# Weight-stationary projections of an encoder layer: of each half weight load, first all products of 512 columns, then all of 256

## The chip, the cores and the metric

One Trainium2 chip, one of its cores. The metric is the device time of one execution of the whole program, in microseconds, as the median of several runs; lower is better. The engines of the core are named as the profile names them: PE (TensorE, matrix products), PEld (the loading of PE's stationary operand), DVE (VectorE), ACT (ScalarE), POOL (GpSimd) and SP (SyncE, which issues most DMAs).

## The reference, cut to what matters

One layer of an encoder over 256 positions of width 2048, all in float32: a mixer of two parallel branches (retention and a gated delta rule) behind one wide input projection, a cross-attention into 256 memory tokens, a squared-ReLU feed-forward of width 8192, and a final norm.

```
h = rms_norm(x, norm_mix_g);  x = x + hybrid_mixer(h, ...)        # w_in: 2048 x 18464, w_out: 2048 x 2048
h = rms_norm(x, norm_x_g);    mem_n = rms_norm(mem, norm_mem_g)
x = x + cross_attention(h, mem_n, w_xq, w_xkv, w_xo)
h = rms_norm(x, norm_ffn_g);  x = x + square(relu(h @ w_ff1)) @ w_ff2
return rms_norm(x, norm_final_g)
```

Nearly all of the work is the matrix products `h @ w`.

## The kernel before

**Products in three parts.** Each float32 operand is split into a rounded part (hi) and the rest (lo), and a product is hi·hi + hi·lo + lo·hi. A weight arrives by DMA in a `raw` tile of 1 MB; `fetch` (L104 on) rounds each half of it on ACT into a tile `whi` (L125) and subtracts on DVE into a tile `wlo` (L126). A half is 128 x 1024 numbers. There are three `raw`, three `whi` and three `wlo` buffers, and later in the program one more pair, `whx` and `wlx`, for every fourth half. The activations lie in "quads", tiles `q` of four feature blocks, each with the 256 hi columns and behind them the 256 lo columns (`both`, 512 columns).

**Two ways to multiply.** `chunk` (L153 on) keeps the activations stationary in PE and streams 512 weight columns, three products of 512 columns for each pair (L166 to L168). `with_seven` (its products at L1185) does the same for the second feed-forward matrix. `values_both` (L401 to L403) does it for the first values of the memory. `blocks_in_steps` (L192 on) is the other way: it keeps a 128 x 128 block of weights stationary and streams activations. For each of the 16 feature blocks `kk` and each of its two output blocks `b`, the hi weights meet all 512 columns of `both` (L210: hi·hi and hi·lo side by side, in the two halves of one PSUM bank), and the lo weights meet the 256 hi columns (L211: lo·hi, added to the first half). When all `kk` are done, L220 and L221 add the two halves of the bank. A pair in this document is one product of L210 and the product of L211 that belongs to it: 2 output blocks x 16 `kk` = 32 pairs in a call, 8 pairs in a half load, and 96 calls, so 384 halves and 3072 pairs in the program. The calls compute the keys of the memory (8 calls, over the quads of the memory, about 97 to 191 us), 8192 columns of the input projection (32 calls), the mixer's output projection (8), the queries and the output projection of the cross-attention (8 each), and the first feed-forward matrix (32).

**Order of the work.** The instructions are put in order at build time by a scheduler with a model of time, within priorities: fetches come first, evacuations next, and small work of the mixer is fitted between the projections' products on PE. `step` and `yield` after each half load let other streams put work in. PE, DVE and ACT each run their own instructions in that order.

**Where the operands lie.** `AT_BLOCKS = (56, 0)` shifts the hi half by 56 numbers (224 bytes) inside its tile in `blocks_in_steps` alone; the other callers of `fetch` use (0, 0). In the built program this gives the following starts, as remainders by 256 bytes within a partition: the blocks of `whi` and `whx` that L210 loads lie at 192, those of `wlo` and `wlx` that L211 loads at 224, and the columns of `q` at 224, except for the four quads of the memory (the keys and the values of the memory), whose columns lie at 0. In L1185 and in L137 to L139 of the cross-attention, both operands lie at 224. In L401 to L403 the loaded operand is a quad of the memory, at 0, and the streamed one a weight at 224.

Of the kernel before, what the change touches and what calls it, by code (L numbers as in the profile page):

```python
# [17 lines left out]
P = 128  # L18
D = 2048
S = 256  # L20
NT = S // P
KT = D // P
# [30 lines left out]
def trunk(ctx: ExitStack, tc: tile.TileContext, x_f, mem_f, positions, lead_f, small_f, w_in, ret_gn_g, w_out, w_xq,  # L53
# [3 lines left out]
    act, vec, pool, pe = nc.scalar, nc.vector, nc.gpsimd, nc.tensor  # L57
# [9 lines left out]
    def stream_ps():  # L67
        s0 = psp.tile([P, 512], F32, name="s0", tag="s0", bufs=2)
        s1 = psp.tile([P, 512], F32, name="s1", tag="s1", bufs=2)
        return s0, s1  # L70
# [24 lines left out]
    def step():  # L95
        if steps and next(steps[0], steps) is steps:
            steps.pop(0)
# [6 lines left out]
    def fetch(pieces, k, n, cuts=1, hold=None, at=(0, 0)):  # L104

        raw = wp.tile([P, k * n], F32, name="raw", tag="raw", bufs=3)
        rv = raw.rearrange("p (k n) -> p k n", k=k)
        with tc.high_priority(offset=100000):
            for off, ap in pieces:
                src = ap.rearrange("(k p) n -> p k n", p=P)  # L110
                for c in range(cuts):
                    ks = slice(c * k // cuts, (c + 1) * k // cuts)
                    fetched.append(nc.sync.dma_start(rv[:, ks, off:off + ap.shape[1]], src[:, ks, :]).ins)
            got = []
            for i in range(2):
                if hold:
                    both = hold().both
                    hi, lo = (both[:, a:a + 2, :].rearrange("p a s -> p (a s)") for a in (0, 2))
                else:
                    hi, lo = (h[:, a:a + k * n // 2] for h, a in zip(half_tiles(), at))  # L120
                src = raw[:, i * k * n // 2:(i + 1) * k * n // 2]
                part = k * n // max(cuts, 2)
                for c in range(0, k * n // 2, part):
                    cs = slice(c, c + part)
                    latest["hi"] = act.activation(hi[:, cs], src[:, cs], AF.Copy).ins  # L125
                    latest["lo"] = vec.tensor_sub(lo[:, cs], src[:, cs], hi[:, cs].bitcast(F32)).ins  # L126
                got.append((hi.rearrange("p (k n) -> p k n", n=n), lo.rearrange("p (k n) -> p k n", n=n)))
            latest["raw"] = fetched[-1]
        return got
# [62 lines left out]
    def blocks_in_steps(quads, w, c0, nb, evac, ends=None):  # L192

        k = 16 // nb
        ps = stream_ps()
        n = nb * P
        for g in range(KT // k):  # L200
            halves = fetch([(0, w[g * k * P:(g + 1) * k * P, c0:c0 + n])], k, n, at=AT_BLOCKS)
            for i in range(k):
                kk = g * k + i
                xh, xhl = quads[kk // 4][0][:, kk % 4, :], quads[kk // 4].both[:, kk % 4, :]
                wh, wl = halves[i // (k // 2)]
                for b in range(nb):
                    bs = slice(b * P, (b + 1) * P)
                    lh, ll = wh[:, i % (k // 2), bs], wl[:, i % (k // 2), bs]
                    with tc.issue_after(ends[-1]) if ends else ExitStack():
                        pe.matmul(ps[b], lh, xhl, start=kk == 0, stop=False)  # L210
                        ins = pe.matmul(ps[b][:, :S], ll, xh, start=False, stop=kk == KT - 1).ins  # L211
                if i % (k // 2) == k // 2 - 1:
                    if ends is not None:
                        ends.append(ins)
                    step()
                    yield
        for b in range(nb):
            with tc.high_priority(offset=50000):
                o = sm.tile([P, S], F32, name="bo", tag="bo", bufs=2)
                act.activation(o, ps[b][:, S:], AF.Copy)  # L220
                vec.tensor_add(o, o, ps[b][:, :S])  # L221
                evac(b, o)

    def blocks(*args):
        for _ in blocks_in_steps(*args):
            pass
# [783 lines left out]
    def residual_pass(quads, w, gain, name, loader=None, between=None):  # L1010
# [4 lines left out]
        for b2 in range(8):  # L1015
            xc = loader(b2) if loader else None
            if b2 % 2 == 0:
                nxt.append(quad_b())

            def evac(b, ps, b2=b2, xc=xc):  # L1020
                k = 2 * b2 + b
                vec.tensor_add(rt[:, k, :], ps, xc[:, b, :] if loader else rt[:, k, :])
                g = gains[:, gain + k:gain + k + 1]
                qh, ql = (a[:, k % 4, :] for a in nxt[-1])
                act.activation(qh, rt[:, k, :], AF.Copy, scale=g)
                vec.scalar_tensor_tensor(ql, rt[:, k, :], g, qh.bitcast(F32), op0=ALU.mult, op1=ALU.subtract)
                sq = xa.tile([P, S], F32, name="sq2", tag="sq2", bufs=2)
                act.activation(sq, rt[:, k, :], AF.Square)
                vec.tensor_add(acc, acc, sq)

            if not between or b2 > 1:
                blocks(quads, w, b2 * 256, 2, evac)
                continue
            first_two.append(blocks_in_steps(quads, w, b2 * 256, 2, evac))
            if b2:
                for which in (0, 0, 0, None, 1, 0, 0, 1, 1, 1, 1):
                    if which is None:
                        between()
                    else:
                        next(first_two[which], None)  # L1040
# [20 lines left out]
    for h in range(XH):  # L1061
# [17 lines left out]
        nb = xa.tile([P, NT], F32, name="nb", tag="nb", bufs=2)  # L1079
# [244 lines left out]
    ends = []  # L1324
# [120 lines left out]
```

## Time and profile before

| What | Value |
|---|---|
| median of 3 runs | 2051.8 us (2050.77 to 2052.64) |
| the profiled execution's own time | 2050.97 us |
| its span, first to last instruction | 2049.2 us |
| PE busy | 2038.1 us, 99% of the span |
| DVE, ACT busy | 1542.9 us, 1153.2 us |
| granted PE clock, mean | 0.999 |
| read from HBM | 389.74 MB, 196 GB/s over the span |

Busy times of PE include products that overlap: the record of a product ends after the next has started, since its columns leave the array while the next ones enter. The time that a product takes up on PE is therefore the distance from its start to the next start. The chain of waits lists instructions that set the end, in order of time, with their share of it (start, duration, engine, output tile, line, count), merged where they follow each other; the timeline lists all instructions by start and duration.

### The profile page before, as it was taken

The page shows a single profiled execution, that of the slowest core. Times are in us where ns is not written, and L with a number is a line of the kernel's source. Part 1 is how long each engine was busy: PE and PEld are TensorE (multiplying, and loading weights), DVE is VectorE, ACT ScalarE, POOL GpSimd, SP SyncE. Part 2 cuts the span into 40 slices and gives each one's busy share as a digit, 9 for nine tenths or more (in the row PEclk, how much of TensorE's full clock was granted, in tenths as well). Part 3 has the DMA queues.
Part 4 walks back from the last instruction along what each step waited for, and adds up shares of the span by engine and source line. Part 5 has one row for each costly group of instructions (what it writes and reads, how often), then busy time and mean ns, then how long its engine had stood idle before and what let it go on. Part 6 is the DMA issues. An engine that isn't in the chain of part 4 may idle for free.

```text
span 2049.2 us, 28493 instructions
## 1 busy us (share of the span) xinstructions
PE 2038.1 (99%) x10850; PEld 1756.6 (86%) x10850; DVE 1542.9 (75%) x2433; ACT 1153.2 (56%) x1871; POOL 36.3 (2%) x50
## 2 busy tenths in 40 slices
PE   9999999999999999999999999999999999999998
PEld 8888888988888888888888899888888888888887
DVE  5887788779667875888557666777868887888785
ACT  6655764575457555755446555555545655655554
POOL 0000000000000000000000000000000000000000
PEclk9999999999999999999999999999999999999999
DMA  9679556555555555555467655569657647555662
GB/s 327 204 253 301 185 183 196 164 185 195 187 168 181 194 196 165 184 182 189 156 206 248 191 180 163 173 180 257 219 169 234 219 159 218 200 199 159 220 217 103
DMA packets 329225, 405.24 MB, mean 198 GB/s; under 512 B 34928, under 2 KB 239360, under 8 KB 328960
## 3 DMA queue, kind: packets, MB, share of 16 engines
q1 hardware_dynamic: 328656, 402.74, 61.1%
q8 instruction: 85, 1.39, 0.3%
q10 hardware_dynamic: 432, 0.69, 0.1%
q14 instruction: 52, 0.43, 0.1%
HBM read 389.74 MB, written 11.55 MB: 196 GB/s over the span
## 4 chain that ended last, share of the span: by engine, by line
PE 96%; DMA 1%; DVE 1%; issue 1%; ACT 1%; SPq 0%; POOLq 0%; POOL 0%; DVEq 0%; ACTq 0%
PE s L210 33%; PE s L211 17%; PE s L167 8%; PE s L168 8%; PE s L166 8%; PE b L1185 7%; PE s L1185 6%; PE s L401 1%; PE s L403 1%; PE s L402 1%; PE b L796 1%; PE b L829 1%; PE b L138 0%; DMA raw<-w_ff 0%; PE b L137 0%
## 5 line engine op out<-in xcount | busy, mean ns | idle before, releaser
L210 PE MATMUL s<-q,whi 128*128 128x512 f32 x2816 | 972.6, 391 | 0.8 <-DVE bo L221 0.6
L126 DVE TENSOR_TENSOR wlo<-raw,whi 128x1024 fp32r<-128x1024 f32 x592 | 722.6, 1222 | 294.9 <-ACT whi L125 288.5
L125 ACT ACTIVATE whi<-raw 128x1024 fp32r<-128x1024 f32 x592 | 627.4, 1060 | 518.9 <-PE s L210 189.2
L211 PE MATMUL s<-q,wlo 128*128 128x256 f32 x2816 | 769.3, 280 | 0.7 <-DVE wlo L126 0.6
L210 PEld LDWEIGHTS s<-q,whi 128*128 128x128 f32 x2816 | 520.8, 188 | 102.9 <-DVE bo L221 0.9
L211 PEld LDWEIGHTS s<-q,wlo 128*128 128x128 f32 x2816 | 528.6, 188 | 13.1 <-DVE wlo L126 1.6
L167 PE MATMUL s<-wlo,q 128*128 128x512 f32 x716 | 281.6, 393 | 0.0
L168 PE MATMUL s<-whi,q 128*128 128x512 f32 x716 | 279.3, 390 | 0.0
L166 PE MATMUL s<-whi,q 128*128 128x512 f32 x716 | 258.9, 390 | 0.0
L166 PEld LDWEIGHTS s<-whi,q 128*128 128x128 f32 x716 | 134.3, 188 | 27.9
L168 PEld LDWEIGHTS s<-whi,q 128*128 128x128 f32 x716 | 134.6, 188 | 26.9
L167 PEld LDWEIGHTS s<-wlo,q 128*128 128x128 f32 x716 | 134.6, 188 | 26.7
L220 ACT ACTIVATE bo<-s 128x256 f32<-128x256 f32 x192 | 72.8, 379 | 107.2 <-PE s L211 107.1
L221 DVE TENSOR_TENSOR bo<-bo,s 128x256 f32<-128x256 f32 x192 | 79.9, 416 | 48.6 <-ACT bo L220 48.3
L125 ACT ACTIVATE whx<-raw 128x1024 fp32r<-128x1024 f32 x56 | 59.3, 1059 | 53.7 <-PE s L210 21.9
L210 PE MATMUL s<-q,whx 128*128 128x512 f32 x256 | 89.2, 389 | 0.0
L126 DVE TENSOR_TENSOR wlx<-raw,whx 128x1024 fp32r<-128x1024 f32 x56 | 68.4, 1221 | 24.6 <-ACT whx L125 24.1
L1185 PE MATMUL s<-whi,q 128*128 128x512 f32 x264 | 85.2, 389 | 0.0
L1185 PE MATMUL b<-whi,q 128*128 128x512 f32 x244 | 78.8, 389 | 0.0
L1206 DVE TENSOR_TENSOR wlo<-rt,whi 128x1024 fp32r<-128x1024 f32 x46 | 56.1, 1223 | 23.3 <-ACT whi L1205 22.5
L211 PE MATMUL s<-q,wlx 128*128 128x256 f32 x256 | 70.5, 280 | 0.0
L1205 ACT ACTIVATE whi<-rt 128x1024 fp32r<-128x1024 f32 x46 | 48.8, 1060 | 33.4 <-PE s L1185 15.3
(385 smaller groups left out, 2344.7 us busy)
## 6 DMA issues: line engine op xcount, KB each, us to landing
raw<-w_in SPq DMA_DIRECT2D x143, 1024.0 KB
raw<-w_ff SPq DMA_DIRECT2D x104, 1024.0 KB
raw<-w_xkv SPq DMA_DIRECT2D x29, 1024.0 KB
raw<-w_out SPq DMA_DIRECT2D x16, 1024.0 KB
raw<-w_xq SPq DMA_DIRECT2D x16, 1024.0 KB
raw<-w_xo SPq DMA_DIRECT2D x16, 1024.0 KB
rt<-w_ff SPq DMA_DIRECT2D x12, 1024.0 KB
tr<-w_ff SPq DMA_DIRECT2D x12, 1024.0 KB
```

The lines of the kernel that those rows point to most:

```text
L125: latest["hi"] = act.activation(hi[:, cs], src[:, cs], AF.Copy).ins
L126: latest["lo"] = vec.tensor_sub(lo[:, cs], src[:, cs], hi[:, cs].bitcast(F32)).ins
L166: pe.matmul(o, xh, wh, start=first, stop=False)
L167: pe.matmul(o, xh, wl, start=False, stop=False)
L168: pe.matmul(o, xl, wh, start=False, stop=last)
L210: pe.matmul(ps[b], lh, xhl, start=kk == 0, stop=False)
L211: ins = pe.matmul(ps[b][:, :S], ll, xh, start=False, stop=kk == KT - 1).ins
L220: act.activation(o, ps[b][:, S:], AF.Copy)
L221: vec.tensor_add(o, o, ps[b][:, :S])
L1185: ins = pe.matmul(o, lhs[l], rhs[r], start=key not in opened, stop=last and j == 2, skip_group_check=True).ins
L1205: latest["hi"] = act.activation(hi, raw[:, c:c + 1024], AF.Copy).ins
L1206: latest["lo"] = vec.tensor_sub(lo, raw[:, c:c + 1024], hi.bitcast(F32)).ins
```

## The change

In each half load, the products of L210 for all four `kk` and both `b` now come first (8 products of 512 columns), and then the 8 products of 256 columns with the lo weights. Before, the two alternated. The products are the same and as many, with the same operands in the same tiles at the same places; only their order differs, and the point in the half at which the lo tile is first read and the hi tile last read. The file is one line shorter, so lines behind it are numbered one lower, and both kinds of product now stand in one line, L210.

```diff
-            for i in range(k):
-                kk = g * k + i
-                xh, xhl = quads[kk // 4][0][:, kk % 4, :], quads[kk // 4].both[:, kk % 4, :]
-                wh, wl = halves[i // (k // 2)]
-                for b in range(nb):
-                    bs = slice(b * P, (b + 1) * P)
-                    lh, ll = wh[:, i % (k // 2), bs], wl[:, i % (k // 2), bs]
-                    with tc.issue_after(ends[-1]) if ends else ExitStack():
-                        pe.matmul(ps[b], lh, xhl, start=kk == 0, stop=False)
-                        ins = pe.matmul(ps[b][:, :S], ll, xh, start=False, stop=kk == KT - 1).ins
-                if i % (k // 2) == k // 2 - 1:
-                    if ends is not None:
-                        ends.append(ins)
-                    step()
-                    yield
+            for h in range(2):
+                for part in range(2):
+                    for i in range(k // 2):
+                        kk = (2 * g + h) * k // 2 + i
+                        x = quads[kk // 4][0] if part else quads[kk // 4].both
+                        for b in range(nb):
+                            o = ps[b][:, :S] if part else ps[b]
+                            with tc.issue_after(ends[-1]) if ends else ExitStack():
+                                ins = pe.matmul(o, halves[h][part][:, i, b * P:(b + 1) * P], x[:, kk % 4, :],
+                                                start=kk == 0 and not part, stop=kk == KT - 1 and part == 1).ins
+                if ends is not None:
+                    ends.append(ins)
+                step()
+                yield
```

The order on PE in the last block of the first feed-forward matrix, before (`s0` and `s1` are the banks of its two output blocks):

```order
L210 MATMUL s0_18055<-q_12127,whi_18059 128x512
L211 MATMUL s0_18055<-q_12127,wlo_18060 128x256
L210 MATMUL s1_18056<-q_12127,whi_18059 128x512
L211 MATMUL s1_18056<-q_12127,wlo_18060 128x256
L210 MATMUL s0_18055<-q_12127,whi_18059 128x512
L211 MATMUL s0_18055<-q_12127,wlo_18060 128x256
```

The same place in the changed program, from the fifth product of the half:

```order
L210 MATMUL s0_18055<-q_12127,whi_18059 128x512
L210 MATMUL s1_18056<-q_12127,whi_18059 128x512
L210 MATMUL s0_18055<-q_12127,whi_18059 128x512
L210 MATMUL s1_18056<-q_12127,whi_18059 128x512
L210 MATMUL s0_18055<-q_12127,wlo_18060 128x256
L210 MATMUL s1_18056<-q_12127,wlo_18060 128x256
L210 MATMUL s0_18055<-q_12127,wlo_18060 128x256
L210 MATMUL s1_18056<-q_12127,wlo_18060 128x256
```

A product of 512 columns was followed by one of 256 and the other way round; now seven of eight are followed by one of their own length.

In the mixer, small products stand between those of the projections. Here are, on PE, the Gram products of the first pair of heads (`kh` and `kl` are the hi and lo parts of a head's keys and queries, made by ACT and DVE), before:

```order
L211 MATMUL s1_2076<-q_110,wlo_2126 128x256
L699 MATMUL b_2189<-kh_2185 128x512
L701 MATMUL b_2190<-kh_2185 128x256
L210 MATMUL s0_2276<-q_107,whi_2280 128x512
L211 MATMUL s0_2276<-q_107,wlo_2281 128x256
L210 MATMUL s1_2277<-q_107,whi_2280 128x512
L211 MATMUL s1_2277<-q_107,wlo_2281 128x256
L210 MATMUL s0_2276<-q_107,whi_2280 128x512
L699 MATMUL b_2189<-kl_2186,kh_2185 128x512
```

And in the changed program:

```order
L210 MATMUL s1_2076<-q_110,wlo_2126 128x256
L698 MATMUL b_2189<-kh_2185 128x512
L700 MATMUL b_2190<-kh_2185 128x256
L210 MATMUL s0_2276<-q_107,whi_2280 128x512
L210 MATMUL s1_2277<-q_107,whi_2280 128x512
L210 MATMUL s0_2276<-q_107,whi_2280 128x512
L698 MATMUL b_2189<-kl_2186,kh_2185 128x512
```

The first product that needs `kl` stood behind five products of the projection, and now stands behind three.

## Prediction

> **What bounds the kernel now.** I read the page's first part, then what PE waited for, then the chain of waits for the pace of PE, then the timeline for single products.
>
> ```profile
> PE 2038.1 (99%) x10850; PEld 1756.6 (86%) x10850; DVE 1542.9 (75%) x2433; ACT 1153.2 (56%) x1871; POOL 36.3 (2%) x50
> PEclk9999999999999999999999999999999999999999
> GB/s 327 204 253 301 185 183 196 164 185 195 187 168 181 194 196 165 184 182 189 156 206 248 191 180 163 173 180 257 219 169 234 219 159 218 200 199 159 220 217 103
> L210 PE MATMUL s<-q,whi 128*128 128x512 f32 x2816 | 972.6, 391 | 0.8 <-DVE bo L221 0.6
> L126 DVE TENSOR_TENSOR wlo<-raw,whi 128x1024 fp32r<-128x1024 f32 x592 | 722.6, 1222 | 294.9 <-ACT whi L125 288.5
> L211 PE MATMUL s<-q,wlo 128*128 128x256 f32 x2816 | 769.3, 280 | 0.7 <-DVE wlo L126 0.6
> L210 PE MATMUL s<-q,whx 128*128 128x512 f32 x256 | 89.2, 389 | 0.0
> L211 PE MATMUL s<-q,wlx 128*128 128x256 f32 x256 | 70.5, 280 | 0.0
> ```
>
> PE is busy for 2038.1 of 2049.2 us, and the clock is full in every slice. The 2816 + 256 = 3072 pairs that the change reorders stood idle for 0.8 + 0.7 us together. So nothing that arrives earlier can win more than 1.5 us in these loops, and the question is only whether PE takes the same products at another pace in another order. The mean durations (391 and 280 ns) are no pace, since products overlap. Pace is the distance from start to start.
>
> ```profile
> 1442.61 21.79 PE b L1185 x96
> 1752.21 2.75 PE b L1185 x12
> 1766.02 2.75 PE b L1185 x12
> 22.71 0.47 PE s L401 x2
> 47.91 0.47 PE s L401 x2
> 123.70 0.47 PE s L210 x2
> 129.28 0.47 PE s L210 x2
> ```
>
> These rows of the chain of waits give four paces.
>
> - An unbroken row of 96 products of 512 columns (L1185) takes 21.79 us: 227.0 ns each.
> - From 1752.21 to 1766.02 us lie 12 products of L1185 (2.75 us) and one block of 32 pairs: 13.81 - 2.75 = 11.06 us, or 345.6 ns a pair. Less 227.0 this leaves 118.6 ns for the product of 256. So today an alternating 512 costs what a 512 costs in an unbroken row.
> - From 22.71 to 47.91 us, in the first values of the memory, lie 9 steps of 12 products of 512 columns (two weight pieces, two token halves, three products): 25.20 us / 108 = 233.3 ns each, 6.3 ns more than in L1185, at the same clock and without idle time.
> - From 123.70 to 129.28 us lies half a block of memory keys, 16 pairs in 5.58 us: 348.8 ns, 3.2 ns more than the later pairs.
>
> What differs in the last two is where the operands lie. PE loads the weights of the next product while the current one streams:
>
> ```profile
> 401.30 0.19 PEld L210 LDWEIGHTS s<-q,whi 128*128 128x128 f32 x1
> 401.30 0.28 PE L211 MATMUL s<-q,wlo 128*128 128x256 f32 x1
> 401.42 0.39 PE L210 MATMUL s<-q,whi 128*128 128x512 f32 x1
> ```
>
> The load for the L210 that starts at 401.42 begins at 401.30, with the L211 before it. So each load runs beside a stream of other data. In L1185 the load and the stream beside it start at the same remainder by 256 bytes (224 and 224): 227.0 ns. In L401 they do not (0 and 224): 233.3 ns. In the later pairs, the load beside the 512 is that of `wlo` (224, stream 224: equal); in the memory keys it is 224 against 0: unequal, and slower. My reading is that a load at another remainder slows the 512 beside it by some 6 ns. The tile that does not fit is `whi` at 192, and today it is always loaded beside the short product.
>
> **The change, step by step.** It adds and removes no product, load, rounding or DMA, and moves no tile. What it swaps is which load runs beside which stream. Take a half of 8 pairs in the later calls.
>
> Today, 8 loads of `wlo` (equal) run beside a 512, and 8 loads of `whi` (unequal) beside a 256: 8 x 345.6 = 2764.8 ns.
>
> After, 7 loads of `whi` (unequal) run beside a 512, one of `wlo` (equal) beside the last 512, 7 of `wlo` (equal) beside a 256, and one of `whi` beside the last 256. For a row of 256 with equal remainders there is this stretch of the cross-attention (timeline):
>
> ```profile
> 1172.82 0.28 PE L137 MATMUL b<-kth,qth 128*128 128x256 f32 x1
> 1172.94 0.28 PE L138 MATMUL b<-ktl,qth 128*128 128x256 f32 x1
> 1173.42 0.28 PE L139 MATMUL b<-kth,qtl 128*128 128x256 f32 x1
> 1173.54 0.39 PE L210 MATMUL s<-q,whi 128*128 128x512 f32 x1
> ```
>
> Six products from 1172.82 to 1173.54 us: 120 ns each, 1.4 above the 118.6 of today. The half becomes 7 x 233.3 + 227.0 + 7 x 120 + 118.6 = 2818.7 ns, 53.9 ns more: 44.1 from the 512s and 9.8 from the 256s.
>
> Of the 384 halves, 32 are those of the memory keys, where the streams start at 0: there `wlo` (224) and `whi` (192) are both unequal, so every load is unequal in either order, and I cost these at nothing. Bound: with the full 53.9 ns it would be 1.7 us.
>
> The sum: 352 x 53.9 ns = 19.0 us. The profiled execution took 2050.97 us (span 2049.2), so 2070.0 us; the median of the runs shown lies 0.8 above it, so **2071 us**.
>
> Prices and their bounds. For a 512 with an unequal load the trace has no long row inside these calls. Upper end, the start of a block, where the scheduler already put two 512s, then two 256s:
>
> ```profile
> 1754.57 0.40 PE L1185 MATMUL b<-whx,q 128*128 128x512 f32 x1
> 1754.81 0.63 PE L210 MATMUL s<-q,whi 128*128 128x512 f32 x2
> 1755.27 0.40 PE L211 MATMUL s<-q,wlo 128*128 128x256 f32 x2
> 1755.52 0.39 PE L210 MATMUL s<-q,whi 128*128 128x512 f32 x1
> 1756.20 0.39 PE L210 MATMUL s<-q,whi 128*128 128x512 f32 x1
> ```
>
> These four take 0.71 us from 1754.81 to 1755.52, the next two pairs 0.68, so one load of `whi` beside a 512 costs up to 0.03 us with the rounding of these rows. The chain rows above have 0.47 us for two 512s there, 235 ns each. With 235 for all 512s and 120 for all 256s a half takes 2840 ns: 352 x 75 = 26.5 us, 2078 us. Lower end, the memory keys' 3.2 ns a pair: 7 x 3.2 = 22 ns a half, 7.9 us, 2060 us. I take 233.3, since it is the pace of 108 products in a row, as the change makes them.
>
> Arrivals. The lo tile is now needed 8 x 0.23 us later than the hi tile, which only loosens the wait on L126 (0.6 us in all). `whi` is free for ACT about 0.95 us earlier, `wlo` when it was. A half takes 2.8 us on PE and its subtraction 1.22 us on DVE, so the rounding stays ahead; its cost is nothing, hidden behind the half before. If that cover were gone, PE would stand for up to those 1.22 us at the start of a half. The evacuation L220 waits for the last 256 of its bank, which for `s0` now comes 0.12 us before the end and not 0.35; the next call has its own two banks, so no product waits for it. The small products of the mixer move by a few products on PE: the first Gram product that needs `kl` now starts 0.23 + 0.12 + 3 x 0.23 = 1.0 us after the first that does not, where it was 1.3.
>
> ```profile
> 614.40 0.69 DVE L694 TENSOR_TENSOR kl<-kq,kh 128x512 fp32r<-128x512 f32 x1
> 614.85 0.39 PE L699 MATMUL b<-kh 128*128 128x512 f32 x1
> 616.14 0.39 PE L699 MATMUL b<-kl,kh 128*128 128x512 f32 x1
> ```
>
> Here (a later pair of heads) `kl` is ready at 615.09 us, 0.24 us after the first Gram product began, so 1.0 us is still enough. I cost the moved small work at nothing, and at up to 3 us for the range.
>
> **The rivals.**
>
> *No price for the order.* The load and the stream do not meet, and the 6.3 ns of L401 belong to the start of the program, where DMAs are dense. Then every product keeps its pace and the time is 2051.8 us, or 2055 with the 1.4 ns on the 256s alone (352 x 9.8 ns = 3.4 us). For it: L401 and the memory keys both lie in the first four of 40 slices, where DMAs move 327, 204, 253 and 301 GB/s. Against it: the 235 ns at 1754.81, and these rows of the chain of waits from the second slice, at 204 GB/s near the mean:
>
> ```profile
> 82.39 0.47 PE s L166 x2
> 93.59 0.47 PE s L166 x2
> ```
>
> Four steps of 12 products, over the memory quads again, take 11.20 us: still 233.3 ns each. The Trainium skill, page "SBUF — State Buffer", section "Who interferes with whom", is on this side: it gives PE two independent read ports, one for the streamed operand and one for the weights, and by it this sum is nothing. The 233.3 against 227.0 ns at a full clock speaks against that rule, but no row before the change separates place from time fully. Chance 0.11.
>
> *Faster.* Rows of equal length could suit PE: if a row of 512s ran at 227.0 whatever is loaded, and a row of 256s at what the memory keys leave for theirs (348.8 - 233.3 = 115.5 ns), a half would take 2740 ns, 24.8 less, and the time would be 352 x 24.8 = 8.7 us lower, 2043 us. It decides as soon as a 256 after a 256 falls under 118.6; the six at 1172.82 take 120, so I give it 0.05.
>
> *New waits.* The price holds and, besides, moved small work of the mixer comes too early for its inputs and stops PE: four groups of heads with some 0.8 us or more each, 2074 us and up. Against it: the scheduler placed it, and the slack shown above. Chance 0.08.
>
> *The change does not do what it says*, because the scheduler mixes the two lengths again. The order on PE shows rows of eight and eight; 0.01, with the time of before.
>
> **How the numbers follow.** The forecast, the price of an unequal load, has 0.75, with 2062 to 2078 us as its own range. The range is 2057 to 2080: the low end lies 3 us under the time by the memory keys' price, the high end the 235 ns with some new waits; no price at all and faster are left out. Differences under 0.2% (4 us) cannot be told from none here. Faster 0.05, within 0.2% 0.11, slower 0.84.
>
> **What would show it.** Right: in the chain or timeline after, eight L210 of 512 columns of a later call span 1.86 us (233 ns each, against 227), eight of 256 some 0.96; a block of 32 pairs between two rows of L1185 takes 11.27 us, not 11.06; the memory keys stay at 5.58 us for 16 pairs; PE's idle time stays at some 11 us. Wrong: 512s at 227 in a row (then the place of the weights does not matter), a loss that sits in idle time of PE, or memory keys that slow as much as the rest.

## The result, and the profile after

The changed kernel takes 2066.93 us (median of 6 runs, 2066.55 to 2067.74), the kernel before beside it 2052.02 us (6 runs, 2050.77 to 2053.05). The ratio is 1.0073, with a 95% interval from 1.0061 to 1.0084: 14.9 us slower.

The page of the kernel after, its first lines and the groups of the changed products and their rounding (group: line, engine, what it does, count, busy us, mean ns of one, idle us before it and what ended that):

```profile
span 2064.8 us, 28550 instructions
PE 2055.3 (100%) x10850; PEld 1759.2 (85%) x10850; DVE 1529.2 (74%) x2433; ACT 1152.3 (56%) x1871; POOL 36.3 (2%) x50
PEclk9999999999999999999999999999999999999999
L126 DVE TENSOR_TENSOR wlo<-raw,whi 128x1024 fp32r<-128x1024 f32 x592 | 721.6, 1221 | 361.0 <-ACT whi L125 352.3
L210 PE MATMUL s<-q,whi 128*128 128x512 f32 x2816 | 720.2, 395 | 0.1
L210 PE MATMUL s<-q,wlo 128*128 128x256 f32 x2816 | 398.7, 282 | 0.0
```

PE works 17.2 us longer (2055.3 against 2038.1) with the same count of products and the same clock, and stands idle 1.6 us less (9.5 us of the span, against 11.1). Together that is the 15.6 us by which the span grew. The idle time in front of the projection's products fell from 0.8 + 0.7 us to 0.1. So nothing waits for anything new; PE is simply slower at the same work. (The busy times of the two groups of L210 fell, since products of one group now overlap with each other; they are no pace.)

The chain of waits of the kernel after shows the pace (start, duration, line, count):

```profile
144.67 47.41 PE s L210 x272
1765.48 2.75 PE b L1184 x12
1768.23 11.26 PE s L210 x64
1971.12 21.79 PE b L1184 x96
```

A block of 32 pairs takes 11.26 us where it took 11.06. A row of L1184 (L1185 before) still takes 21.79 us for 96 products. The keys of the memory take 47.41 us for 136 pairs, 348.6 ns each, as before (348.8). And the timeline of the kernel after splits a block into its rows:

```profile
1596.23 2.02 PE L210 MATMUL s<-q,whi 128*128 128x512 f32 x8
1598.09 1.11 PE L210 MATMUL s<-q,wlo 128*128 128x256 f32 x8
1599.04 2.03 PE L210 MATMUL s<-q,whi 128*128 128x512 f32 x8
```

Eight 512s span 1.86 us from start to start (1598.09 - 1596.23), 233 ns each, and eight 256s 0.95 us, 119 ns each. Before, eight of each took 8 x 227.0 = 1.82 and 8 x 118.6 = 0.95 us; so nearly the whole loss lies in the products of 512.

### The profile page after: what moved, and what is told of

It reads as the page before. It is cut to its first block, busy times and chain, and to the rows that moved or that the text cites. A ratio compares the mean times of both kernels' runs of the same rounds, so it can differ in the third digit from the quotient of the medians.

```text
span 2064.8 us, 28550 instructions
## 1 busy us (share of the span) xinstructions
PE 2055.3 (100%) x10850; PEld 1759.2 (85%) x10850; DVE 1529.2 (74%) x2433; ACT 1152.3 (56%) x1871; POOL 36.3 (2%) x50
## 4 chain that ended last, share of the span: by engine, by line
PE 98%; DVE 1%; DMA 1%; issue 0%; ACT 0%; POOLq 0%; POOL 0%; ACTq 0%
PE s L210 52%; PE s L167 8%; PE s L168 8%; PE s L166 8%; PE b L1184 7%; PE s L1184 6%; PE s L400 1%; PE s L401 1%; PE s L402 1%; PE b L795 1%; PE b L698 1%; PE b L828 1%; PE b L138 1%; PE b L137 0%; PE b L139 0%; DMA raw<-w_ff 0%
## 5 line engine op out<-in xcount | busy, mean ns | idle before, releaser
L210 PE MATMUL s<-q,whi 128*128 128x512 f32 x2816 | 720.2, 395 | 0.1
L210 PEld LDWEIGHTS s<-q,whi 128*128 128x128 f32 x2816 | 503.1, 188 | 95.8 <-DVE q L134 0.3
L210 PEld LDWEIGHTS s<-q,wlo 128*128 128x128 f32 x2816 | 386.5, 189 | 32.7
L210 PE MATMUL s<-q,wlo 128*128 128x256 f32 x2816 | 398.7, 282 | 0.0
L168 PE MATMUL s<-whi,q 128*128 128x512 f32 x716 | 279.3, 390 | 0.0
L168 PEld LDWEIGHTS s<-whi,q 128*128 128x128 f32 x716 | 134.5, 188 | 27.3
L1184 PE MATMUL s<-whi,q 128*128 128x512 f32 x264 | 85.2, 389 | 0.0
L1184 PE MATMUL b<-whi,q 128*128 128x512 f32 x244 | 78.8, 389 | 0.0
L220 DVE TENSOR_TENSOR bo<-bo,s 128x256 f32<-128x256 f32 x192 | 71.9, 412 | 0.0
L657 DVE SCALAR_TENSOR_TENSOR acc<-bo,small,acc 128x255 f32<-128x255 f32 (+2 forms) x144 | 60.7, 478 | 7.3 <-ACT acc L654 7.3
L210 PE MATMUL s<-q,whx 128*128 128x512 f32 x256 | 64.9, 395 | 0.0
L219 ACT ACTIVATE bo<-s 128x256 f32<-128x256 f32 x192 | 61.9, 372 | 3.6 <-PE s L210 3.4
```

The lines of the kernel that those rows point to most:

```text
L168: pe.matmul(o, xl, wh, start=False, stop=last)
L210: ins = pe.matmul(o, halves[h][part][:, i, b * P:(b + 1) * P], x[:, kk % 4, :], start=kk == 0 and not part, stop=kk == KT - 1 and part == ...
L657: vec.scalar_tensor_tensor(acc[:, d:], ps[:, :S - d], cw[:, j, blk:blk + 1], acc[:, d:], op0=ALU.mult, op1=ALU.add)
L1184: ins = pe.matmul(o, lhs[l], rhs[r], start=key not in opened, stop=last and j == 2, skip_group_check=True).ins
```

## The experiments

In all of them "equal" means that the weight block that is loaded and the columns that stream beside it start at the same remainder by 256 bytes. The yardstick beside the time is a block of 32 pairs in the first feed-forward matrix, between two rows of L1184 or L1185: 11.06 us before, 11.26 after. Where pairs stand in rows, the chain of waits has it as one line of 64 products; where they alternate, it is the distance of two rows of 12 less the first row's duration.

### The changed order with equal places

```diff
-AT_BLOCKS = (56, 0)
+AT_BLOCKS = (0, 0)
```

> The changed order, with the shift of the hi tile taken out, so that whi is loaded at 224 like the streams. Theory of place (a weight load whose start differs from that of the stream by a remainder of 256 bytes slows a 512-column stream): a row of eight 512s goes from 233.5 to 227 ns each, a row of 256s stays at 119, a half falls by some 46 ns, 352 halves by 16 us: 2050 to 2053 us, the time of before. Rival, the order itself (two 512s in a row cost more, wherever the weights lie): 233 ns and 2067 us stay. Rival, a part of each: 2057 to 2062 us.

2060.11 us, ratio 1.0039 (1.0024 to 1.0054): half of the loss goes, half stays, the third of the three answers. In the chain of waits a block takes 11.15 us; the timeline shows a half:

```profile
1762.43 11.15 PE s L210 x64
```

```profile
1400.87 2.00 PE L210 MATMUL s<-q,whx 128*128 128x512 f32 x8
1402.71 1.12 PE L210 MATMUL s<-q,wlx 128*128 128x256 f32 x8
1403.66 2.00 PE L210 MATMUL s<-q,whi 128*128 128x512 f32 x8
```

Eight 512s take 1.84 us, still more than 8 x 0.227 = 1.816. Taken from start to start over the 295 halves without other work between, the eight 512s take 233, 235, 228, 232, 230, 227, 227 and 227 ns, nearly the same in every half. So with equal places a row of 512s does reach 227, but only after five products; in the change they stay at 232 to 234 throughout. The equal place is one cause, and something that the 256s leave behind is another.

Fourteen rows of the later calls in this kernel stand behind products of 512 columns (L168 or L1184) and not behind 256s. They run at 226.7 ns on average, from the first product on. The timeline at such a place, with the next row of the same block:

```profile
1762.05 0.39 PE L1184 MATMUL b<-whx,q 128*128 128x512 f32 x1
1762.27 1.98 PE L210 MATMUL s<-q,whi 128*128 128x512 f32 x8
1764.09 1.11 PE L210 MATMUL s<-q,wlo 128*128 128x256 f32 x8
1765.04 2.00 PE L210 MATMUL s<-q,whi 128*128 128x512 f32 x8
1766.88 1.12 PE L210 MATMUL s<-q,wlo 128*128 128x256 f32 x8
```

The row behind L1184 takes 1.82 us, the row behind 256s 1.84.

### The order of before, with the other tile shifted

The shift moves from the hi tile to the lo tile, in both kinds of buffer (the other two places that make `whi` and `wlo` tiles change their sizes in the same way):

```diff
-AT_BLOCKS = (56, 0)
+AT_BLOCKS = (0, 56)
-                         for nm, room in (("whx", 128), ("wlx", 0)))
+                         for nm, room in (("whx", 0), ("wlx", 128)))
-        return tuple(wp.tile([P, 1024 + room], F32R, name=nm, tag=nm, bufs=3) for nm, room in (("whi", 64), ("wlo", 0)))
+        return tuple(wp.tile([P, 1024 + room], F32R, name=nm, tag=nm, bufs=3) for nm, room in (("whi", 0), ("wlo", 64)))
```

> The order of before, alternating, with the shift of 224 bytes moved from the hi tile to the lo tile: the load beside each 512 (lo) is now at 192 against 224, the load beside each 256 (hi) at 224 against 224. Theory of place: the 512s go from 227.4 to some 232 ns although nothing is put in rows, 2816 x 5 ns = 14 us more, 2064 to 2069 us. Rival, the order itself: 2052 us as before, within 3 us.

2070.64 us, ratio 1.0092 (1.0075 to 1.0109): as slow as the change and more, with no order changed. In the chain of waits of this kernel:

```profile
1768.03 2.77 PE b L1185 x12
1782.07 2.77 PE b L1185 x12
```

14.04 - 2.77 = 11.27 us a block. The 512s take 232.7 ns, as the theory of place has it, and the 256s 120.2, which it did not foresee. A loss of this size needs no rows. That the unequal lo loads cause it is not shown by this run: with both tiles at equal places ("The alternating order, with all places equal") the alternating 512s take 234.7 ns.

### The changed order, with the other tile shifted

The same edit in the changed kernel.

> The changed order with the shift on the lo tile: hi loads beside 512s at 224 against 224, lo loads beside 256s at 192 against 224. Theory of place: 512s at 227 ns in a row; the 256s lose the small cost of an equal load (119 to 117.5 ns), so 2048 to 2051 us, 1 to 4 us under the unshifted one. Rival, the order itself: 2064 to 2067 us.

2056.49 us, ratio 1.0018 (1.0008 to 1.0028), between the two answers and outside both. The chain of waits:

```profile
1758.62 11.10 PE s L210 x64
```

The 512s start a row as in the first experiment (232, 235, 228, 231, 230, 227, 227 ns) and end it with one of 235, beside which the first lo tile is loaded, now unequal. The 256s with unequal loads take 116.6 ns on average, against 119.0 in the first experiment. So the eighth 512 does as the theory says, and the slow start of each row stays.

### The change, with other neighbours in the bank

```diff
-                    for i in range(k // 2):
-                        kk = (2 * g + h) * k // 2 + i
-                        x = quads[kk // 4][0] if part else quads[kk // 4].both
-                        for b in range(nb):
+                    for b in range(nb):
+                        for i in range(k // 2):
+                            kk = (2 * g + h) * k // 2 + i
+                            x = quads[kk // 4][0] if part else quads[kk // 4].both
```

> The changed order, but within each part first the four products of one output block, then the four of the other, so that the bank changes once in four products and no product streams the same columns as the one before it. Loads and places as in the change. Theory of place: 233 ns and 2065 to 2069 us stay. Rivals, a change of bank at every product, or the same columns streamed twice in a row, as the cause of the 6 ns: back to 2050 to 2056 us.

2068.82 us, ratio 1.008 (1.0065 to 1.0095), and a block in the chain of waits as in the change:

```profile
1770.69 11.26 PE s L210 x64
```

Neither the change of bank at every product nor streaming the same columns twice in a row plays a part.

### Rows of four, with equal places

```diff
-                for part in range(2):
-                    for i in range(k // 2):
+                for part, i0 in ((0, 0), (1, 0), (0, k // 4), (1, k // 4)):
+                    for i in range(i0, i0 + k // 4):
```

> The unshifted changed order, but in rows of four: 4 products of 512, 4 of 256, twice a half. Theory of settling (with equal places, the first five 512s after a row of 256s still take 233, 235, 228, 232 and 230 ns, whatever the weights' place, and only then 227): two settlings a half instead of one, 2 x 928 = 1857 ns of 512s a half and not 1840, some 6 us more than the unshifted rows of eight, 2064 to 2068 us. Rival, the 24 ns a half have another cause that does not come with each switch: 2058 to 2061 us.

2066.95 us, ratio 1.0074 (1.0058 to 1.0089), and in the chain of waits:

```profile
1768.08 11.20 PE s L210 x64
```

Against 11.15 in rows of eight. The 512s take 234, 234, 232 and 229 ns, 928 in four, the sum that the first four of a row of eight take. The slow start comes with each switch from 256s to 512s.

### Other distances

The change with shifts of 32 and of 128 bytes (`AT_BLOCKS = (8, 0)` and `(32, 0)`). They put the hi blocks at 0 and at 96, so 32 and 128 bytes from the streams at 224. In the change they lie at 192, which is 32 bytes away on the other side.

> The change with a hi shift of 32 bytes: whi at 0, streams at 224 (the distance of the first values of the memory). Theory of place, any unequal remainder costs the same: 512s in a row at 233 ns, 2064 to 2069 us. Rival, the price grows with the distance: other than at 192, by more than 2 us.

> The change with a hi shift of 128 bytes: whi at 96, streams at 224, half of 256 bytes apart. Theory of place, any unequal remainder costs the same: 512s in a row at 233 ns, 2064 to 2069 us. Rival, the price goes by the distance: 512s at 236 ns and more, or near 227.

2064.94 us with 32 bytes and 2063.18 with 128, one run each beside 2052.57 for the kernel before. From the chains of waits, first 32 bytes, then 128:

```profile
1766.74 11.23 PE s L210 x64
```

```profile
1765.13 11.21 PE s L210 x64
```

The eight 512s sum to 1863 and 1862 ns, against 1865 in the change: at 128 bytes the price is the same as at 32. It is not the same everywhere: in the memory keys of the changed kernel, where the hi loads are 64 bytes from the streams (192 against 0), the first seven 512s average 229.9 ns. What differs is the 256s (118.0 and 117.4 ns, against 118.9), and that puts the second a little under its expectation.

The kernel with 32 bytes also has equal places other than 224. In its memory keys, `whi` and the streams both start at 0, and `wlo` at 224. The timeline of two halves there:

```profile
131.72 2.01 PE L210 MATMUL s<-q,whi 128*128 128x512 f32 x8
133.56 1.10 PE L210 MATMUL s<-q,wlo 128*128 128x256 f32 x8
134.50 2.01 PE L210 MATMUL s<-q,whi 128*128 128x512 f32 x8
```

From start to start the 512s take 232, 235, 229, 232, 231, 227, 227 and 235 ns on average over 25 halves, nearly the same as in the changed order with the other tile shifted, where the equal place is 224. So it is the equality that counts in a row, and not the place 224 itself.

### The kernel before, with the memory's quads at an equal place

```diff
-PAD1, PAD2 = 144, 80
+PAD1, PAD2 = 136, 80
```

> The kernel before, with the pad ahead of the memory's quads 32 bytes shorter, so that they lie at 224 like all others: in the values of the memory loads and streams are now equal, and in the keys the lo loads beside the 512s. Theory of place: the 512s of the first 97 us go from 233.3 to 227 (436 x 6.3 ns = 2.7 us), the pairs of the keys from 348.8 to 345.6 ns (256 x 3.2 = 0.8 us): 3.5 us less if PE sets the pace there, 2048 to 2049.5 us. Rival, the start of the program is slow for other reasons (dense DMAs): 2052 us, and 233 ns stay.

2049.57 us against 2052.57 beside it, ratio 0.9988 (0.9979 to 0.9997): 3.0 us faster than the kernel before, the best version here. From its timeline, at the time of the rows of L401 that the prediction read:

```profile
19.77 0.39 PE L401 MATMUL s<-whi,q 128*128 128x512 f32 x1
19.99 0.39 PE L402 MATMUL s<-wlo,q 128*128 128x512 f32 x1
20.22 0.39 PE L403 MATMUL s<-whi,q 128*128 128x512 f32 x1
```

From start to start 0.22 and 0.23 us; over 20 to 95 us the products of 512 take 226.8 ns on average, where they took 233.3 at the same time of the program with the same DMAs. The streamed weights of L401 to L403 stayed where they were; the quads moved, and so did the tiles allocated behind the pad, all by 32 bytes. And the chain of waits, in the keys:

```profile
122.32 0.46 PE s L210 x2
136.15 0.46 PE s L210 x2
```

40 pairs in 13.83 us, 345.8 ns each and no longer 348.8. In the profiled executions the last L210 of the keys starts 2.0 us earlier (189.15 us against 191.16), and the span is 1.5 us shorter, so the gain arises in this part of the program. The rival by which the start of the program is slow for other reasons falls.

### The alternating order, with other shifts

The kernel of the last experiment with the hi tile shifted by 128 and by 32 bytes.

> The alternating order of before with the memory's quads at 224 (as in e8), and the hi tile shifted by 128 bytes instead of 224, so that whi, loaded beside the 256s, lies at 96. Theory of place: lo loads beside the 512s stay equal, so 227 ns there; the 256s may change by 1 ns either way, 3 us: 2046 to 2053 us, against 2049.6 for e8. Rival, the shift of 224 is the only good one: over 2053 us.

> As e9, with a shift of 32 bytes: whi at 0. Theory of place: 512s at 227 ns, 2046 to 2053 us. Rival, the shift of 224 is the only good one: over 2053 us.

2067.07 us, ratio 1.0072 (1.0058 to 1.0086), and 2064.54 us, ratio 1.0061 (1.0048 to 1.0074). Both expectations of the theory of place missed by over 11 us: the lo load beside each 512 is equal, and the 512s still take 233 to 234 ns. The chains of waits, first 128 bytes:

```profile
1766.09 2.79 PE b L1185 x12
1780.14 2.79 PE b L1185 x12
```

```profile
1763.51 2.75 PE b L1185 x12
1777.50 2.75 PE b L1185 x12
```

11.26 and 11.24 us a block. So the place of the hi load, which runs beside a 256 and carries the weights of the 512 after it, counts too. No run here tells whether it counts as a neighbour of the 256 or as the 512's own weights. Of the four places tried for it (192, 224, 0, 96; the second stands below) only 192 lets the alternating 512s run at 227 ns.

### The alternating order, with all places equal

`AT_BLOCKS = (0, 0)` in the kernel before.

> The kernel before, alternating, with the hi shift taken out: every load of the later calls at 224, like the streams. Theory of place alone (only the load beside a 512 counts): 512s stay at 227 ns, 256s go from 118 to 119.5, 2816 x 1.5 ns = 4 us more at most, 2052 to 2057 us. Theory with settling (after a 256 with an equal load the next 512s take 233 to 235 ns, as the first five of a row do): every 512 follows such a 256, 512s at 231 to 235 ns, 2064 to 2070 us.

2065.12 us, ratio 1.0063 (1.0046 to 1.008), as settling has it: the 512s average 234.7 ns. This kernel also shows two rhythms for the same instructions. From its chain of waits, two products that lie 72 pairs apart, and from its timeline, two that lie six pairs apart:

```profile
1404.67 0.23 PE s L210
1429.63 0.23 PE s L210
```

```profile
1930.60 0.40 PE L210 MATMUL s<-q,whi 128*128 128x512 f32 x1
1932.72 0.40 PE L210 MATMUL s<-q,whi 128*128 128x512 f32 x1
```

The 24.96 us of the first are 346.7 ns a pair; the 2.12 us of the second are 353.3. Within such a stretch the distances repeat to within 1 ns (231, 112, 233, 117 ns in the one; 232, 118, 240, 120, 236, 114 in the other), and the stretches looked at keep one rhythm for tens of pairs. Neither reaches the 345.6 ns of the kernel before.

### Rows of two, with the shift of the change

```diff
-                for part in range(2):
-                    for i in range(k // 2):
+                for part, i in [(p, j) for j in range(k // 2) for p in range(2)]:
+                    if True:
```

> The change with its shift of 224 bytes, but in rows of two: for each feature block two 512s, then two 256s. Half of the hi loads run beside a 512 and not seven of eight. Theory of place: the price goes with their number, 4 x 6.3 ns a half and some 6 ns from the 256s, 352 x 31 ns = 11 us, 2060 to 2065 us, under the change. Rival, any order other than strict alternation costs the same: 2066 to 2069 us.

2057.52 us, ratio 1.0027 (1.0016 to 1.0038), less than expected: the 512s average 229.7 ns, some 0.7 less than the theory gives, and the 256s cost nothing more (117.1 ns on average). A block in the chain of waits:

```profile
1760.67 11.11 PE s L210 x64
```

The direction holds: rows of two cost less than rows of eight. The reason does not. Of each two 512s, the first has the unequal hi load beside it and the second the equal lo load, so by the theory they take 233 and 227 ns. From start to start they take 230.2 and 229.2 on average over the later calls. In this order the load beside a 512 does not set that product's own pace.

## Why the prediction was right, and where its reason fell short

**The bound** (PE's own pace, no waits): right. Idle time fell, and all of the loss is busy time.

**The price of the 512s** (7 x 6.3 ns a half): right in size. The eight 512s of a half went from 1818.0 to 1864.8 ns, taken from start to start over the 221 and 295 halves without other work between: 46.8 ns, forecast 44.1. Some 4 to 5 ns of it lie in the eighth 512, beside which the equal lo tile is loaded: it takes 231.9 ns, where the sum had 227.0.

**The price of the 256s** (9.8 ns a half): 7.8 (943.5 to 951.3).

**The block and the memory keys**: 11.26 us, forecast 11.27; 348.6 ns a pair, forecast 348.8.

**The sum**: 19.0 us was forecast and 14.9 measured, 15.6 in the spans. Of the difference, 1.6 us is the idle time that went away, about the 1.5 us that I had named as the most that arrivals could win. Part of the rest is that I counted 352 halves as strictly alternating before the change. They were not all: the scheduler had already put two 512s side by side at the start of many blocks and between small work. Before, the 100 later 512s with a 512 ahead of them and a 256 behind took 232.2 ns, and the 2520 between two 256s 227.4. So some of the price had been paid, by my estimate from these and similar rows about 1 us of it. PE's busy time grew by 17.2 us and not by 19.0; the remainder is not broken down.

**Moved small work**: right at nothing; no wait on it appears in the profile after.

**The reason**: this is the step that fell short. It said that a load at another remainder slows the 512 beside it by some 6 ns, and by implication that a 512 with an equal load runs at 227. The first half is shown for rows: the memory's quads, moved by 32 bytes, took the 512s of L401 to L403 from 233.3 to 226.8 ns. It does not hold product by product in every order, as the rows of two show (230.2 and 229.2 ns). And the 232.7 ns with the lo tile shifted in the order of before met the forecast by luck, since there both tiles at equal places gave 234.7. The second half is not true. With equal places the rows of 512s behind 256s still begin with five slow products, rows of four are slow throughout, and the alternating order with equal places is slower than with the shift. In these runs the 512s average 227 ns in two situations only: in a row of equal loads, at once behind other 512s and after some five products behind 256s, and in strict alternation with the lo load equal and the hi load at 192. The change left the second situation and reached, with its places, neither. With equal places it would still have lost, 8 us of its 15, to the slow starts. My one price thus stood for two causes that do not add: where the loads are unequal the 512s are at 233 already, and the slow start does not show.

The terms of the sum, 7 x 233.3 + 227.0, fit the rows of the change that stand behind 512s: in 13 of these 14 the eighth 512 takes 226 or 227 ns. Behind 256s, where nearly all rows stand, it takes 232. The lines that the prediction read already held the sign. Of the two 512s that start at 1754.81 us, the second has the equal lo load beside it, as the timeline of PEld before shows:

```profile
1755.04 0.42 PEld L211 LDWEIGHTS s<-q,wlo 128*128 128x128 f32 x2
```

Yet in the trace both 512s take 233 ns from start to start. The price of a block came out right because in the change nearly every 512, with an equal load beside it or not, takes about what the prediction had for an unequal one.

**The rivals.** That the order costs nothing is out (1.0061 to 1.0084). The Trainium skill's page "SBUF — State Buffer", section "Who interferes with whom", stood on that side: it gives PE two independent read ports, one for the stream and one for the weights. By it alone the place of a weight load would not matter to a stream; 233.3 against 226.8 ns in L401 to L403 speaks against taking that as the whole account. Faster 256s exist (116.6 ns in rows with unequal loads, against 117.9 before), but the slower 512s beside them cost more than they give. New waits did not come.

**Open**: what a row of 256s, or a 256 with an equal load, leaves behind that takes five products to wear off; why alternation runs at 227 ns with the hi tile at 192 and at none of the other places tried; and what picks one of the two rhythms. Rows of sixteen, which would have halved the switches, were not tried.

## What to carry to other kernels

On a kernel that PE bounds, a new order of products is priced from the distances from start to start in its own trace, and a few nanoseconds a product are the whole budget: 5 ns on 3072 pairs are 15 us. Look at where the weights and the streamed columns start: here a pad of 32 bytes was worth 3 us, and a shift that helps one order has to be chosen again for another. Do not expect a price found in one neighbourhood of instructions to be complete: test the place and the order apart, as the equal places here gave back only half.

## What the runs showed of the hardware that was not expected

- At full clock and with no wait, products of 512 columns took 227 ns in some orders and places, and 229 to 235 on average in others; it depended on where weights and streamed columns start, to 32 bytes, and on the products before.
- With equal places, a row of 512s ran at 227 ns from the first product behind other 512s, and behind 256s only after five products of 228 to 235 ns.
- Unequal places 32 bytes to either side and 128 bytes away gave sums of 1863, 1865 and 1862 ns for eight (the first and the last from one run each).
- In strict alternation the place of the hi tile, loaded beside the 256s, set the pace of the 512s: with the lo load equal, hi at 192 gave 227 ns, at 0, 96 and 224 it gave 233 to 235.
- The same alternating instructions at the same places settled into two different steady rhythms, 346.7 and 353.3 ns a pair, in one execution.
